# A two-layer trunk on one core: weights' splits held at the end of attention and of x's pairs, x loaded in four pieces, k's last part on VectorE

## Chip, core and metric

The kernel runs on one core of one Trainium2 chip. The metric is device time in microseconds (us) of one execution. All data are fp32 in HBM; the whole trunk runs in one launch.

## What is computed

A decoder trunk of two layers for one sequence of 256 positions, width 1024, feed-forward width 2816. Each layer adds half of a gated feed-forward block, then a mixer, then half of another feed-forward block; every block reads x through an RMS norm with its own gain, and a last norm follows. The mixer of layer 0 is, side by side, an attention of 8 heads of 64 whose three dilated windows are combined by their softmax sums, and a gated mixing of 4 groups of 128 positions by 128; layer 1 has a causal attention of 16 heads.

```
def swiglu(x, w_gate, w_up, w_down):
    return (jax.nn.silu(x @ w_gate) * (x @ w_up)) @ w_down
...
    h = x
    for layer in range(DEPTH):
        h = h + 0.5 * swiglu(rms_norm(h, ffn1_norm[layer]),
                             ffn1_w_gate[layer], ffn1_w_up[layer], ffn1_w_down[layer])
        hn = rms_norm(h, mix_norm[layer])
        if layer % 2 == 0:
            i = layer // 2
            h = h + ab_mixer(hn, ab_w_in[i], ab_v_norm[i], ab_w_spatial[i],
                             ab_b_spatial[i], ab_w_out[i])
        else:
            i = layer // 2
            h = h + c_mixer(hn, c_w_in[i], c_w_out[i])
        h = h + 0.5 * swiglu(rms_norm(h, ffn2_norm[layer]),
                             ffn2_w_gate[layer], ffn2_w_up[layer], ffn2_w_down[layer])
    return rms_norm(h, final_norm)
```

## The kernel before

**Engines.** TensorE (PE) multiplies and transposes, VectorE (DVE) and ScalarE (ACT) do the elementwise work, GpSimd (POOL) some of it, SyncE (SP) issues the loads.

**Three matmuls for one.** Each fp32 operand is split into a high part, rounded to the matmul's format, and a low part, the remainder. `mm3` (L223 to L226) multiplies high by high (L224), the weight's high by the other operand's low (L225), and the weight's low by the other's high (L226). For a 128 x 128 weight tile the moving operand has 256 columns, the positions.

**The weight stream.** `Stream` (L49 to L139) carries all weights through SBUF in chunks of 2048 columns by 128 partitions, 1 MB, in the order in which they are used. A chunk is loaded on SP's queue into one of 3 raw buffers (`load_one`, L72), then split by `split_one` into a high part (L105, ACT) and a low part (L106, DVE), in two or more pieces, into one of 4 pairs of buffers. `take` hands out the next chunk, `free` gives its buffers back, and both call `pump`, which issues every load and every split that the buffers allow at that point of the program. So a chunk's splits stand in the engines' order wherever a `free` happened to allow them. Chunks marked `reset` are laid out otherwise and split in more pieces (two of 384 columns first).

**Order on an engine.** The tile scheduler sets each engine's order, by the program's order and the dependences; only `begin` is written out by hand. `tc.issue_after` places the instructions that are made within it behind a given one on its engine.

**Phases.** ffn, mixer of layer 0 (`ab_mixer`), ffn, ffn, mixer of layer 1 (`c_mixer`), ffn. x is held transposed (features on partitions) as eight tiles of 128 x 256; `xTh` and `xTl` are its gained high and low parts for the next block. A block's norm is applied behind the matmuls, by `norm["row"]`, so that the next block's matmuls can begin before the sum of squares is known.

**End of a mixer.** `project` (L339 to L372) multiplies the mixer's output by w_out in two halves; each half fills two banks of PSUM, each bank a pair of x tiles. `Next.pair` (L265 to L289) takes such a pair: it adds x (L269, DVE), makes the two high parts (L259, ACT) and low parts (L262, DVE), squares (L279, ACT) and adds to the sum of squares (L283 to L289, DVE). The next ffn's first chunk (its order, `LATE`, leaves x's last two tiles for the end) starts right behind.

**Attention in `ab_mixer`.** `make_attention` (L623 to L714) gives five functions. `put_k` (L655) scales a pair of k heads (DVE), copies each head's high part (L661, ACT) and subtracts for its low part (L662, POOL). `scores` (L668) makes one head's scores (L677, L678, PE), adds the mask and takes the maximum (L681, DVE), exponentiates (L684, ACT), inverts the sum (L687, DVE) and scales (L691: POOL, but DVE for the last four heads). `turn` (L694) transposes a head's probabilities (L699, PE) and splits them (L229, ACT, and L230, DVE). `weighted` (L704) multiplies a pair of heads with v. `Slots` (L722) runs these at numbered steps of the projections' matmuls, so that PE has other work while a head goes through the engines: the last four heads' scores at 20, 20, 21, 21, their `turn` at 22, 22, 23, 23, and the last two `weighted` at 24 and 25, all within the first half of `project`.

**Begin.** `begin` (L375 to L456) loads x in rows of positions, as two tiles `xr`, and transposes it (L423) into four banks of two x tiles each; from these ACT and DVE take high and low parts (L259, L262) before any norm. Two halves of x's columns are loaded, each as two pieces of 128 x 512, ahead of the first and the third of four pieces of the first weight chunk. `heat` (L396) puts matmuls of zeros on PE; `turn_gains` (L401) transposes one of the three gain arrays and copies it (L405, DVE) into `gT`. Each of four steps waits for its two x tiles and its piece of the weight and does all three matmuls for them. The gains of the mixers and of the second ffn are transposed behind the third chunk of the first ffn.

Of the kernel before, what the change touches and what calls it, by code (L numbers as in the profile page):

```python
# [48 lines left out]
class Stream:  # L49


    def __init__(self, nc, pools):
        self.nc, (self.raw_pool, self.hi_pool, self.lo_pool) = nc, pools
        self.specs, self.raws, self.parts = [], {}, {}
        self.loaded = self.split = self.done = self.next = 0

# [62 lines left out]
    def pump(self):  # L119
        n = len(self.specs)  # L120
        while True:
            if self.loaded < n and self.loaded - RAW < self.split:
                self.load_one()
            elif self.split < self.loaded and self.split - SPL < self.done:
                self.split_one()
            else:
                break

# [14 lines left out]
def trunk(ctx: ExitStack, tc: tile.TileContext, a, out):  # L143
# [44 lines left out]
    add_ffn(a["ffn1_w_gate"][0], a["ffn1_w_up"][0], a["ffn1_w_down"][0], again=(1, 3, 5))  # L188
# [39 lines left out]
    def split(hi, lo, src):  # L228
        nc.scalar.activation(hi, src, AF.Copy)  # L229
        nc.vector.tensor_sub(lo, src, hi.bitcast(F32))  # L230
# [14 lines left out]
    class Next:  # L245
# [15 lines left out]
        def lo(self, k, src):  # L261
            nc.vector.scalar_tensor_tensor(xT["l"][:, k], src, self.gain(k), xT["h"][:, k].bitcast(F32),  # L262
                                           op0=ALU.mult, op1=ALU.subtract)

        def pair(self, i, p, row=None, pool=None):  # L265
# [10 lines left out]
            for k in (2 * i, 2 * i + 1):  # L276
                self.lo(k, X[:, k])
            q = wk.tile([128, 2, S], F32, name="sq" if i else "acc", bufs=1)
            nc.scalar.activation(q, xs, AF.Square, scale=1.0 / math.sqrt(D))  # L279
# [7 lines left out]
            if i == 3:  # L287
                for j in range(2):
                    nc.vector.tensor_add(f, f, q[:, j])  # L289

# [48 lines left out]
    def project(mix, order, phase, after):  # L339
# [35 lines left out]
    def begin(fp):  # L375

        nonlocal nxt
        xr = [fp.tile([128, D], F32, name=f"xr{t}") for t in range(NT)]
# [11 lines left out]
        nc.scalar.dma_start(*grs[0])  # L390
# [19 lines left out]
        for g in grs[1:]:  # L410
            nc.sync.dma_start(*g)
# [5 lines left out]
        p = bank()  # L417
        for i in range(4):
            if i < 2:
                for t in range(NT):  # L420
                    for k in range(4 * i, 4 * i + 4):
                        c = k % 2 * S + t * 128
                        nc.tensor.transpose(px[k // 2][:, c : c + 128], xr[t][:, k * 128 : (k + 1) * 128], ident)  # L423
                if i == 0:
                    heat(HEAT1)
            src = both(px[i])
            nxt.hi(2 * i, src[:, 0])
            nxt.lo(2 * i, src[:, 0])
            next(parts)
            nxt.hi(2 * i + 1, src[:, 1])  # L430
            nxt.lo(2 * i + 1, src[:, 1])
            w = st.parts[0]
            for k in (2 * i, 2 * i + 1):
                for j in range(2):
                    cs = slice(j * 128, (j + 1) * 128)
                    mm3(p[:, j * S : (j + 1) * S], w[0][k][:, cs], w[1][k][:, cs], xT["h"][:, k], xT["l"][:, k],
                        k == 0 and j == 0, k == KD - 1 and j == 1)
# [6 lines left out]
        for t in range(NT):  # L444
            xs = [xr[t][:, h * 512 : (h + 1) * 512] for h in range(2)]
# [10 lines left out]
        return p, turn_gains  # L456

    def ffn(phase):
        nonlocal nxt
        with tc.tile_pool(name="fp", bufs=1) as fp:  # L460
# [29 lines left out]
            for n in range(FT):  # L490
                k, m = n - n % 2, n % 2
                if phase == n == 0:
                    with tc.manual_schedule():
                        p, turn_gains = begin(fp)
# [10 lines left out]
                if phase == 0 and n == 2:  # L505
                    turn_gains(1)
                    turn_gains(2)
# [115 lines left out]
    def make_attention(mp, mask_cols, nheads, v, mix, rows=False):  # L623
# [31 lines left out]
        def put_k(p, bk):  # L655

            t = scaled(bk)
            for j in range(2):
# [3 lines left out]
                nc.gpsimd.tensor_sub(k[o, :], t[r, :], k[r, :].bitcast(F32))  # L662
# [5 lines left out]
        def scores(h):  # L668
# [10 lines left out]
            for b, (c0, n) in enumerate(((0, 128), (128, 256))):  # L679
# [4 lines left out]
                nc.scalar.activation(pr[:, cs], pr[:, cs], AF.Exp, bias=nm[:, b : b + 1], scale=-1.0,  # L684
                                     accum_out=l[:, b : b + 1])
            rl = wk.tile([128, 2], F32, name="rl")
            nc.vector.reciprocal(rl, l)  # L687
            for b, (c0, n) in enumerate(((0, 128), (128, 256))):
                cs = slice(c0, c0 + n)
                engine = nc.gpsimd if h < nheads - 4 else nc.vector  # L690
                engine.tensor_scalar(pr[:, cs], pr[:, cs], rl[:, b : b + 1], None, op0=ALU.mult)  # L691
            probs[h] = pr

        def turn(h):  # L694
# [7 lines left out]
            split(pts[p][0][:, j, :], pts[p][1][:, j, :], tp[:, :384])  # L702

        def weighted(p):  # L704
# [5 lines left out]
            for j in range(2):  # L710
                r = slice(j * 64, j * 64 + 64)
                split(mix[0][r, p], mix[1][r, p], o[r, j, :].rearrange("p (t c) -> p t c", t=NT))
# [86 lines left out]
    def ab_mixer(phase):  # L799
        with tc.tile_pool(name="mp", bufs=1) as mp:  # L800
# [142 lines left out]
```

## Time and profile before

| | us |
|---|---|
| median of 3 executions | 945.18 |
| lowest and highest | 945.04, 945.36 |
| the profiled execution | 944.62 |
| its span, first to last instruction | 942.9 |
| around the span | 1.72 |

The granted clock of TensorE was 0.999 over the span. The page of the profile gives busy times of PE (matmuls), PEld (weight loads, which overlap them), DVE, ACT, POOL and SP, counts behind an x, and groups of instructions by line of the program with their operands as output <- inputs. In a timeline a row is start, duration, engine, line, operation, operands, shape and count; in square brackets stands the idle time ahead of it and what ended it. In a list of waits the numbers are the total, the count and the longest. Matmuls overlap: a matmul's row lasts 0.28 us, but the next can start much earlier, so the distance between starts says how fast PE goes.

### The profile page before, as it was taken

Reading aid. Unit: us, or ns where it says so; the run is one execution under the profiler, and the core shown is the slowest. Engines: PE = TensorE matmul, PEld = TensorE weight load, DVE = VectorE, ACT = ScalarE, POOL = GpSimd, SP = SyncE. Lnnn points to the kernel's source line nnn. Section 1 sums busy time; section 2 is a strip of 40 time slices with the busy share of each in tenths; the row PEclk is TensorE's granted clock in tenths of the full one; section 3 lists DMA queues with packets and bytes.
Section 4 is the critical chain, followed back from the end, with each engine's and each line's share of the span. In section 5 each row is a group of like instructions: output and inputs, shape, how many; then the busy total and the mean of one; then the engine's idle time right before and its main releaser. Section 6 shows DMA issues by size and latency. Waiting matters only on the chain.

```text
span 942.9 us, 18152 instructions
## 1 busy us (share of the span) xinstructions
PE 933.5 (99%) x7685; PEld 911.5 (97%) x7685; DVE 607.5 (64%) x879; ACT 502.1 (53%) x790; POOL 83.4 (9%) x114
## 2 busy tenths in 40 slices
PE   9999999999999999999999999999999999999997
PEld 9999999999999999999999999999999999999886
DVE  6866556677886656655755665566787865666543
ACT  7754444468676445444554544456786755444431
POOL 0000000034400000000000000002574000000000
PEclk9999999999999999999999999999999999999999
DMA  9866555665447566556656655656544476556521
GB/s 305 277 207 196 172 194 172 224 221 179 135 135 221 182 185 210 176 170 203 220 180 188 210 184 171 197 186 215 178 136 136 133 230 195 179 180 201 201 90 44
DMA packets 153537, 174.86 MB, mean 185 GB/s; under 512 B 3008, under 2 KB 142192, under 8 KB 153456
## 3 DMA queue, kind: packets, MB, share of 16 engines
q1 hardware_dynamic: 151888, 171.54, 56.6%
q10 hardware_dynamic: 1568, 2.17, 0.7%
q8 instruction: 60, 0.98, 0.4%
q14 instruction: 21, 0.17, 0.0%
HBM read 172.65 MB, written 1.05 MB: 184 GB/s over the span
## 4 chain that ended last, share of the span: by engine, by line
PE 69%; DVE 2%; ACT 1%; issue 1%; POOLq 0%; POOL 0%; ACTq 0%
PE bank L224 21%; PE bank L225 21%; PE bank L226 20%; PE bank L545 2%; PE bank L549 2%; PE bank L546 2%; DVE wlo L106 1%; PE bank L699 1%; PE bank L677 0%; PE bank L678 0%; ACT whi L105 0%; DVE xTl L262 0%; PE bank L475 0%; DVE pr L691 0%; DVE pr L681 0%
## 5 line engine op out<-in xcount | busy, mean ns | idle before, releaser
L105 ACT ACTIVATE whi<-raw 128x1024 fp32r<-128x1024 f32 (+4 forms) x352 | 331.1, 985 | 366.1 <-issue 282.7
L106 DVE TENSOR_TENSOR wlo<-raw,whi 128x1024 fp32r<-128x1024 f32 (+4 forms) x352 | 390.3, 1141 | 134.9 <-ACT whi L105 133.7
L224 PE MATMUL bank<-xTh,whi 128*128 128x256 f32 x1632 | 452.5, 277 | 0.0
L225 PE MATMUL bank<-xTl,whi 128*128 128x256 f32 x1632 | 451.6, 277 | 0.3 <-DVE xTl L262 0.3
L226 PE MATMUL bank<-xTh,wlo 128*128 128x256 f32 x1632 | 451.2, 276 | 0.2 <-DVE wlo L106 0.2
L225 PEld LDWEIGHTS bank<-xTl,whi 128*128 128x128 f32 x1632 | 306.5, 188 | 0.9 <-DVE xTl L262 0.8
L226 PEld LDWEIGHTS bank<-xTh,wlo 128*128 128x128 f32 x1632 | 306.4, 188 | 0.6 <-DVE wlo L106 0.4
L224 PEld LDWEIGHTS bank<-xTh,whi 128*128 128x128 f32 x1632 | 306.5, 188 | 0.2 <-ACT whi L105 0.2
L224 PE MATMUL bank<-hTh,whi 128*128 128x256 f32 x528 | 145.7, 276 | 0.0
L225 PE MATMUL bank<-hTl,whi 128*128 128x256 f32 x528 | 145.7, 276 | 0.0
L226 PE MATMUL bank<-hTh,wlo 128*128 128x256 f32 x528 | 145.7, 276 | 0.0
L226 PEld LDWEIGHTS bank<-hTh,wlo 128*128 128x128 f32 x528 | 99.1, 188 | 0.0
L224 PEld LDWEIGHTS bank<-hTh,whi 128*128 128x128 f32 x528 | 99.1, 188 | 0.0
L225 PEld LDWEIGHTS bank<-hTl,whi 128*128 128x128 f32 x528 | 99.1, 188 | 0.0
L486 DVE TENSOR_TENSOR hm<-gs,bank 128x512 f32<-128x512 f32 x44 | 30.2, 687 | 79.7 <-PE bank L226 79.3
L483 DVE TENSOR_TENSOR gs<-bank,row 128x512 f32<-128x512 f32 x44 | 30.0, 689 | 47.7 <-PE bank L226 47.7
L224 PE MATMUL bank<-mixh,whi 128*128 128x256 f32 x128 | 35.2, 280 | 0.0
L225 PE MATMUL bank<-mixl,whi 128*128 128x256 f32 x128 | 35.1, 277 | 0.0
L226 PE MATMUL bank<-mixh,wlo 128*128 128x256 f32 x128 | 35.0, 277 | 0.0
L631 POOL MEMSET ql<- 64x256 f32 x12 | 3.7, 309 | 342.1 <-DVE x L273 341.7
L546 PE MATMUL bank<-wlo,hTh 128*128 128x512 f32 x80 | 31.1, 389 | 0.0
L545 PE MATMUL bank<-whi,hTh 128*128 128x512 f32 x80 | 31.1, 389 | 0.0
(139 smaller groups left out, 865.3 us busy)
## 6 DMA issues: line engine op xcount, KB each, us to landing
raw<-in_ffn_w_gate SPq DMA_DIRECT2D x42, 1024.0 KB, 5.3
raw<-in_ffn_w_up SPq DMA_DIRECT2D x42, 1024.0 KB, 5.4
raw<-in_ffn_w_down SPq DMA_DIRECT2D x35, 1024.0 KB, 5.1
raw<-in_c_w_in SPq DMA_DIRECT2D x12, 1024.0 KB, 5.2
raw<-in_ab_w_in SPq DMA_DIRECT2D x10, 1024.0 KB, 5.1
raw<-in_ffn_w_down SPq DMA_DIRECT2D x12, 768.0 KB, 4.5
raw<-in_ab_w_out SPq DMA_DIRECT2D x4, 1024.0 KB, 5.0
raw<-in_c_w_out SPq DMA_DIRECT2D x4, 1024.0 KB, 5.0
```

What stands on the lines that cost most here:

```text
L105: nc.scalar.activation(hi, r, AF.Copy)
L106: nc.vector.tensor_sub(lo, r, hi.bitcast(F32))
L224: nc.tensor.matmul(p, sh, mh, start=start, stop=False)
L225: nc.tensor.matmul(p, sh, ml, start=False, stop=False)
L226: nc.tensor.matmul(p, sl, mh, start=False, stop=stop)
L483: nc.vector.tensor_mul(g, both(pg), twice(norm["row"]))
L486: nc.vector.tensor_mul(hm, g, both(pu))
L545: nc.tensor.matmul(banks[t, h], sh, w[0][kw][:, cs], start=k == 0, stop=False)
L546: nc.tensor.matmul(banks[t, h], sh, w[1][kw][:, cs], start=False, stop=False)
L549: nc.tensor.matmul(banks[t, h], sl, w[0][kw][:, cs], start=False, stop=k == FT - 1)
L631: nc.gpsimd.memset(t[o, SHIFT + j * S : SHIFT + (j + 1) * S].bitcast(F32), 0.0)
L699: nc.tensor.transpose(tp[:, i * 128 : (i + 1) * 128], pr[:, i * 128 : (i + 1) * 128], ident)
```

## The change

It has five parts.

1. The stream can be held: `pump` then issues loads but no splits. `release` splits one chunk, or ends the hold, with the splits placed behind given instructions. In `ab_mixer` the stream is held from slot 19; one chunk is split behind the last head's exponential and scaling, one behind head 5's transposed split, and the rest behind the last `weighted`. In `project`, of both mixers, it is held before the third chunk is freed, and released behind the last pair's square and low part.
2. One chunk of the first ffn, the fourth, is split in two pieces of 1024 columns and no longer in four.
3. x is one tile, loaded in four pieces of 256 columns for both blocks of positions, one ahead of each piece of the first weight chunk. Two gain loads move from SP's queue to ACT's, at the start.
4. In `begin` the transposes of x stand two steps ahead of their use, a step's matmuls with the weight's low part stand behind the next transposes, the gains of the later blocks are transposed at the third step, and one transpose and one matmul of zeros go to a bank of their own at the end.
5. In `ab_mixer`, k's last pair is subtracted on DVE and no longer on POOL, and heads 4 and 5 are scaled on POOL and no longer on DVE.

```
+            elif not self.held and self.split < self.loaded and self.split - SPL < self.done:
                 self.split_one()
...
+    def hold(self):
+
+        self.held = True
+
+    def release(self, tc, behind, one=False):
+
+        with ExitStack() as s:
+            for b in behind:
+                s.enter_context(tc.issue_after(b.ins))
+            if one:
+                self.split_one()
+            else:
+                self.held = False
+                self.pump()
...
-    add_ffn(a["ffn1_w_gate"][0], a["ffn1_w_up"][0], a["ffn1_w_down"][0], again=(1, 3, 5))
+    add_ffn(a["ffn1_w_gate"][0], a["ffn1_w_up"][0], a["ffn1_w_down"][0], again=(1, 5))
...
         for pr in range(2):
             nxt.pair(pr, banks[pr])
+        st.hold()
         st.free()
         w = st.take()
         for pr in (2, 3):
...
-            nxt.pair(pr, banks[pr])
+            added = nxt.pair(pr, banks[pr])
+        st.release(tc, added)
         st.free()
...
         def load_x(i):
-            if i % 2 == 0:
-                h = i // 2
-                for t in range(NT):
-                    nc.sync.dma_start(xr[t][:, h * 512 : (h + 1) * 512],
-                                      x[t * 128 : (t + 1) * 128, h * 512 : (h + 1) * 512])
+            cs = slice(i * S, (i + 1) * S)
+            nc.sync.dma_start(xr[:, :, cs], x[:, cs].rearrange("(t p) c -> p t c", p=128))
...
-        nc.scalar.dma_start(*grs[0])
+        for g in grs:
+            nc.scalar.dma_start(*g)
...
+        turn_x(0)
+        heat(HEAT1)
+        turn_x(1)
         for i in range(4):
+            src = both(px[i])
+            for j in range(2):
+                nxt.hi(2 * i + j, src[:, j])
+            for j in range(2):
+                nxt.lo(2 * i + j, src[:, j])
+            next(parts)
+            w = st.parts[0]
+            tiles = [(k, j, p[:, j * S : (j + 1) * S], slice(j * 128, (j + 1) * 128))
+                     for k in (2 * i, 2 * i + 1) for j in range(2)]
+            for k, j, o, cs in tiles:
+                nc.tensor.matmul(o, w[0][k][:, cs], xT["h"][:, k], start=k == j == 0, stop=False)
+                nc.tensor.matmul(o, w[0][k][:, cs], xT["l"][:, k], start=False, stop=False)
             if i < 2:
...
+                turn_x(i + 2)
+            elif i == 2:
+                turn_gains(1)
+                turn_gains(2)
+            for k, j, o, cs in tiles:
+                nc.tensor.matmul(o, w[1][k][:, cs], xT["h"][:, k], start=False, stop=k == KD - 1 and j == 1)
+        e = bank()
+        nc.tensor.transpose(e[:, :128], warm, ident)
+        nc.tensor.matmul(e[:, 128:S], warm, ident, start=True, stop=True)
...
-                if phase == 0 and n == 2:
-                    turn_gains(1)
-                    turn_gains(2)
...
-                nc.gpsimd.tensor_sub(k[o, :], t[r, :], k[r, :].bitcast(F32))
+                engine = nc.vector if p == 3 and not rows else nc.gpsimd
+                engine.tensor_sub(k[o, :], t[r, :], k[r, :].bitcast(F32))
...
-                engine = nc.gpsimd if h < nheads - 4 else nc.vector
+                engine = nc.gpsimd if h < nheads - (4 if rows else 2) else nc.vector
...
-            slots.at((6, 7, 8, 9, 20, 20, 21, 21), scores)
-            slots.at((10, 10, 12, 12, 22, 22, 23, 23), turn)
-            slots.at((13, 14, 24, 25), weighted)
+            slots.at((19,), lambda _: st.hold())
+            slots.at((6, 7, 8, 9, 20, 20, 21), scores)
+            slots.at((21,), lambda _: st.release(tc, scores(7), True))
+            slots.at((10, 10, 12, 12, 22), turn)
+            slots.at((22,), lambda _: st.release(tc, turn(5), True))
+            slots.at((23, 23), lambda i: turn(6 + i))
+            slots.at((13, 14, 24), weighted)
+            slots.at((25,), lambda _: st.release(tc, weighted(3)))
```

`scores`, `turn`, `weighted`, `split` and `pair` now return the instructions behind which `release` places the splits.

More of the change, by code (lines that the diff above doesn't have):

```diff
@@ L289, in pair @@
                     nc.vector.tensor_add(f, f, q[:, j])
+            return square, low
         def sums(self):
@@ L417, in begin, with turn_x @@
         p = bank()
-        for i in range(4):
-            if i < 2:
[L420 to L437, printed above, removed]
+        def turn_x(i):
+            for k in (2 * i, 2 * i + 1):
+                for t in range(NT):
+                    c = k % 2 * S + t * 128
+                    nc.tensor.transpose(px[i][:, c : c + 128], xr[:, t, k * 128 : (k + 1) * 128], ident)
+        turn_x(0)
+        heat(HEAT1)
+        turn_x(1)
+        for i in range(4):
+            src = both(px[i])
[10 more added lines that the diff above has]
+                nc.tensor.matmul(o, w[0][k][:, cs], xT["l"][:, k], start=False, stop=False)
+            if i < 2:
+                turn_x(i + 2)
[7 more added lines that the diff above has]
+        nc.tensor.matmul(e[:, 128:S], warm, ident, start=True, stop=True)
         for _ in parts:
```

35 lines of the change are left out of this document (17 added, 18 removed).

## The prediction

> **What bounds the kernel now.** I read the page's span, engine shares and chain first, then what TensorE (PE) waited for, then its instructions one by one where it paused.
>
> ```profile
> span 942.9 us, 18152 instructions
> PE 933.5 (99%) x7685; PEld 911.5 (97%) x7685; DVE 607.5 (64%) x879; ACT 502.1 (53%) x790; POOL 83.4 (9%) x114
> PE 69%; DVE 2%; ACT 1%; issue 1%; POOLq 0%; POOL 0%; ACTq 0%
> ...
> PE bank L699 <- DVE pr L691: 1.3, 1, 1.3
> ...
> PE bank L225 <- DVE xTl L262: 0.3, 1, 0.3
> ```
>
> PE is busy 933.5 of 942.9 us. The change takes away no matmul, so all it can win lies in the other 9.4 us (some of it before the first transposes) and in stretches where PE counts as busy but issues at less than its pace. Those do not show as waits; they show as start-to-start distances. In the rows below (start, duration, engine) 282.43 to 282.77 is three matmuls: 0.113 us each, the pace of a fed PE.
>
> ```profile
> 262.49 0.82 PE L699 MATMUL bank<-ident,pr 128*128 128x128 f32 x6
> ...
> 263.27 0.28 PE L225 MATMUL bank<-mixl,whi 128*128 128x256 f32 x1
> ...
> 265.89 0.49 PE L699 MATMUL bank<-ident,pr 128*128 128x128 f32 x3
> 267.68 0.61 PE L699 MATMUL bank<-ident,pr 128*128 128x128 f32 x3 [1.29 <-DVE pr L691]
> ...
> 268.25 0.28 PE L225 MATMUL bank<-mixl,whi 128*128 128x256 f32 x1
> ...
> 282.43 0.28 PE L224 MATMUL bank<-xTh,whi 128*128 128x256 f32 x1
> ...
> 282.77 0.28 PE L224 MATMUL bank<-xTh,whi 128*128 128x256 f32 x1
> ...
> 284.10 0.28 PE L224 MATMUL bank<-xTh,whi 128*128 128x256 f32 x1
> ...
> 754.43 0.28 PE L224 MATMUL bank<-xTh,whi 128*128 128x256 f32 x1
> ...
> 755.51 0.28 PE L225 MATMUL bank<-xTl,whi 128*128 128x256 f32 x1
> ...
> 758.79 0.28 PE L226 MATMUL bank<-xTh,wlo 128*128 128x256 f32 x1
> ...
> 760.06 0.28 PE L224 MATMUL bank<-xTh,whi 128*128 128x256 f32 x1
> ```
>
> Four places: the transposes of heads 6 and 7 (265.89 to 268.25), and three where an FFN has just begun behind a mixer and reads x's last tiles.
>
> **Attention's end, A.** Six transposes and a matmul took 263.27 − 262.49 = 0.78 us for heads 4 and 5, and 268.25 − 265.89 = 2.36 for heads 6 and 7: 1.58 lost, to VectorE (DVE), which scaled head 7 late. The rows say with what it was busy:
>
> ```profile
> 262.78 1.22 DVE L106 TENSOR_TENSOR wlo<-raw,whi 128x1024 fp32r<-128x1024 f32 x1
> ...
> 267.25 0.55 DVE L691 TENSOR_SCALAR pr<-pr,rl 128x128 f32<-128x128 f32 x2
> ...
> L106 DVE TENSOR_TENSOR wlo<-raw,whi 128x1024 fp32r<-128x1024 f32 x12 | 14.4, 1219 | 3.5 <-ACT whi L105 3.4
> L230 DVE TENSOR_TENSOR ptl<-bank,pth 128x384 fp32r<-128x384 f32 x4 | 2.0, 548 | 0.0
> ...
> 253.97 1.54 POOL L662 TENSOR_TENSOR k<-qk,k 64x256 fp32r<-64x256 f32 x2 [0.33 <-ACT k L661]
> 255.73 2.28 POOL L662 TENSOR_TENSOR k<-qk,k 64x256 fp32r<-64x256 f32 x2 [0.22 <-ACT k L661]
> ...
> L691 POOL TENSOR_SCALAR pr<-pr,rl 128x256 f32<-128x256 f32 x16 | 17.8, 1112 | 0.0
> L691 POOL TENSOR_SCALAR pr<-pr,rl 128x128 f32<-128x128 f32 x16 | 10.1, 630 | 20.2 <-DVE rl L687 14.4 <-PE bank L699 5.5
> ```
>
> Two chunks' low halves, four L106 of 1.22 us (group mean 1219 ns), stood ahead of head 7's scaling, which ended at 267.25 + 0.55 = 267.80. With both chunks held that end moves to at most 267.80 − 4 × 1.22 = 262.9, 3.0 us before PE asks at 265.89: the whole 1.58 goes. Heads 4 and 5's scaling moves to POOL, 2 × (1.11 + 0.63) = 3.5 us; k's last two subtractions leave POOL (255.73 to 258.01), so I start it at 257.9 with head 4's sums and end near 261.4, against PE's 262.49: 1.1 us of cover. What was held must still be in time. The first chunk's splits run behind head 7's exponentials and scaling, by my count to 265.2, for a matmul at about 275. The second's stand behind head 5's transposes, to 268.3; the lows of heads 6 and 7 follow, 2 × 0.55 behind it, at 269.3, and the last `weighted` reads them, by my count, at about 270.7 (1.4 us of cover).
>
> The new cost is k's last two subtractions, on DVE from about 254.7, beside POOL's for the pair before (253.97 to 255.51), whose second part scores(5) waits for on PE. One POOL subtraction costs 1.54 / 2 = 0.77 with little beside it; the later two, 2.28 in all, ran partly beside a DVE L106. Two more of them undisturbed would be 1.54, so DVE cost POOL 0.74 there. DVE's two new ones are shorter than that L106: between nothing and 0.85 later; I take +0.25. A: −1.58 + 0.25 = **−1.33** (−1.58 to −0.73).
>
> The Trainium skill, SBUF — State Buffer, section Who interferes with whom, speaks against this edit: of a VectorE instruction with two SBUF inputs and a GpSimd one that reads SBUF, the second to come is blocked until the first has ended. L662's 2.28 beside L106 against 1.54 agrees. By that rule POOL's subtraction could wait for both of DVE's and A would be −0.73.
>
> **Pairs, B.** Distances against 0.113 per step: 282.77 to 284.10 is 9 steps, 1.33 − 1.02 = 0.31; 754.43 to 755.51 is 7, 1.08 − 0.79 = 0.29; 758.79 to 760.06 is 7 (one record is missing from the order L224, L225, L226), 1.27 − 0.79 = 0.48. Together 1.08, all where the lows of x's last pairs come late behind a chunk's splits:
>
> ```profile
> 756.46 2.42 DVE L106 TENSOR_TENSOR wlo<-raw,whi 128x384 fp32r<-128x384 f32 x3
> 758.80 0.87 DVE L262 SCALAR_TENSOR_TENSOR xTl<-x,gT,xTh 128x256 fp32r<-128x256 f32 x2
> ```
>
> Holding the next chunks until pair 3's low and square are issued puts this 2.42 behind the 0.87, so tile 7's low is ready near 756.46 + 0.87 = 757.3, and PE asks at 758.9. In the first mixer one chunk's lows (2 × 1.22) now stand ahead of the adds of pairs 0 and 1; I count pair 2's lows 0.45 us ahead of PE, the thinnest cover here, and if it fails the 0.31 stays or doubles. The held chunks end about 3 us ahead of their matmuls; their loads are issued up to 5 us later on SP, whose queue holds only loads, and the next chunk still lands 1 us or more before it is split. B: **−1.08** (−1.1 to −0.5).
>
> **The begin, C.** Rows: transposes, first matmul, the second weight chunk's first matmul, then the groups for 4 to 14 us (count, busy, mean ns), and the gains' place in the old order.
>
> ```profile
> 4.18 1.42 PE L423 MATMUL bank<-ident,xr 128*128 128x128 f32 x8
> ...
> 6.47 0.39 PE L224 MATMUL bank<-xTh,whi 128*128 128x256 f32 x1
> ...
> 13.78 0.28 PE L224 MATMUL bank<-xTh,whi 128*128 128x256 f32 x1
> ...
> 24.59 0.28 PE L226 MATMUL bank<-xTh,wlo 128*128 128x256 f32 x1
> ...
> 25.24 0.28 PE L225 MATMUL bank<-xTl,whi 128*128 128x256 f32 x1
> ...
> L262 DVE SCALAR_TENSOR_TENSOR xTl<-bank,gT,xTh 128x256 fp32r<-128x256 f32 x8 | 3.7, 480 | 2.3 <-ACT xTh L259 2.3
> L259 ACT ACTIVATE xTh<-bank,gT 128x256 fp32r<-128x256 f32 x8 | 3.6, 473 | 3.9 <-PE bank L423 3.6 <-DVE xTl L262 0.2
> ...
> L106 DVE TENSOR_TENSOR wlo<-raw,whi 128x512 fp32r<-128x512 f32 x4 | 2.8, 693 | 0.1
> ...
> L405 DVE COPY gT<-bank 128x16 f32<-128x16 f32 x1 | 0.2, 173 | 3.2 <-PE bank L404 3.2
> ```
>
> The 48 matmuls cost 48 × 0.113 = 5.4 us in either order, and the last eight transposes lie among them in either. What sets the end is DVE, with two lows and a split per step: 2 × 0.48 + 0.69 = 1.65, four times, 6.6 us. After: first transposes end near 5.15, the first high half 0.47 later, then 6.6, plus two gain copies that now stand in DVE's order (2 × 0.17): 12.6 if nothing else waits. The copies wait for PE's gain transposes, which stand behind the third step's matmuls, so I add 0.7: 13.3; then the last four matmuls and two fillers, 0.45 + 0.33: the next chunk starts near 14.1, +0.37. In return the gains leave 24.59 to 25.24, 0.65 for two steps of 0.23: −0.42. C: **0** (−0.6 to +0.6). x's four pieces are needed by PE at about 4.2, 5.9, 7.5 and 9.3. Before, x's second half, issued at 2.7 and 3.2, took 4.3 and 5.3 us to land (the row below: shortest, median, longest), at 7.0 and 8.5, and the same bytes lie ahead of it now:
>
> ```profile
> DMA to landing us min/median/max: 4.3/4.8/5.3
> ```
>
> so I count no wait for x. One chunk of the first FFN gets 2 + 2 splits for 4 + 4 on engines that are not the bound there: nothing. The two gain loads go from SP to ScalarE's queue, ahead of anything it does: nothing.
>
> **Sum.** −1.33 − 1.08 + 0 = −2.41. The profiled execution took 944.62 (span 942.9 and 1.72 around it), so 942.2 there; the median shown, 945.18, is 0.56 above it: **942.8**.
>
> **Rivals.** 1, **attention's wait is exchanged**: POOL, given heads 4 and 5 and slowed by DVE beside it, ends past 262.49, or its k subtraction is held by 0.85, and PE waits there in place of at head 7. For: 1.1 us of cover against POOL groups of 1.11 and 0.63. Against: POOL loses its 2.28 us of k. It leaves A at about −0.2 and the sum at −1.3: 943.9. 2, **x lands late**: PE's order now puts transposes of pieces 2 and 3 ahead of low-half matmuls, so a late piece stops ready ones. If pieces keep arriving 1.5 us apart, as those two did, the third comes some 1.2 us late: sum −1.2, 944.0. 3, **slower**: the start's transfers as a whole slow down, from runs of 1 KB in x's rows in place of 2 KB:
>
> ```profile
> 0.00:5.00 5.00, 3.90 (x17) 1.00 0.57 183
> 5.00:10.00 5.00, 4.77 (x40) 1.00 0.99 324
> 10.00:15.00 5.00, 5.00 (x43) 1.00 1.09 349
> ```
>
> (Length, PE busy and its count, granted clock, DMA share, GB/s of each stretch.) x, the first and the second weight chunk are 3.15 MB, and PE wants the last of it by about 13.6. From the first issue at 0.8 that is 246 GB/s on the mean, and below it PE waits: at 183 GB/s all the way they take 17.2 us, to 18.0, and PE stands 4.4 us: −2.4 + 4.4 = +2.0, 947.2. Against: 324 and 349 GB/s as soon as the queue is full. 4, **the begin gains**: with DVE and ACT fed earlier the step pauses (13.78 − 6.47 = 7.31, less 5.4 and 0.9 of transposes: 1.0 idle) vanish: −0.9 more, 941.9. 5, the order does not change what is late: 0, 945.2.
>
> **How the numbers follow.** The forecast 0.61; rival 1 0.12, rival 2 0.12, rival 4 0.08, rival 3 0.05, rival 5 0.02. The bounds of A, B and C added in the same direction would be −3.3 to −0.6; not all fall together. The range 941.2 to 944.4 takes in rivals 1, 2 and 4 and leaves out 3, 5 and the tails: about 2 in 10. About 0.2% (1.9 us) is what a measurement of this kernel can tell from no change, so faster means below 943.3: 0.53 of the forecast's own 0.61, and rival 4: 0.61. Within: the forecast's other 0.08 and rivals 1, 2 and 5: 0.34. Slower: rival 3, 0.05.
>
> **What would show it.** Right: transposes of heads 6 and 7 with no wait on DVE's pr (A); a wait of scores on POOL's k of some 0.25 us more; no wait on xTl behind either mixer and distances of 0.113 there (B); the second chunk's first matmul at 14.1, with DVE's gain copies followed by a pause of the fourth step, and no gain transposes near 24.6 (C). Wrong: PE waiting for POOL's pr of head 4 or 5 (rival 1), transposes waiting for x's pieces (2), the second chunk's matmuls waiting for its split behind a late landing (3), or the last `weighted` waiting for held lows, which I counted 1.4 us clear.

## The result and the profile after

The changed kernel takes 942.66 us (median of 10 executions, 942.21 to 943.19) against 945.2 (10, 944.85 to 945.88): ratio 0.9972, 95% interval 0.9962 to 0.9982, 2.54 us faster. The forecast was 942.8. Its profiled execution took 942.51, 2.11 less than the one shown of before. On the page, the share of DVE in the chain of work that ended last has gone from 2% to nothing.

```profile
span 940.8 us, 18159 instructions
PE 932.5 (99%) x7688; PEld 911.1 (97%) x7688; DVE 608.5 (65%) x875; ACT 501.8 (53%) x788; POOL 83.9 (9%) x116
...
PE 71%; issue 1%; ACT 0%; DVE 0%; POOL 0%; POOLq 0%
```

What PE waited for (total, times, longest): the waits on DVE's `pr` and `xTl` are gone, and two new ones stand in their place, on a piece of x and on POOL's k. The wait of 1.1 us at the start was there before.

```profile
PE bank L415 <- DVE warm L408: 1.1, 1, 1.1
PE bank L437 <- DMA xr<-in_x: 0.6, 1, 0.6
PE bank L702 <- POOL k L687: 0.3, 1, 0.3
```

**Where the time went.** The first products of gates and norm in each ffn (`gs`, on DVE) follow PE's matmuls without slack, so their starts say how far PE is, at four places: in the first ffn, behind the first mixer, in the third ffn, behind the second mixer. Before:

```profile
39.49 1.28 DVE L483 TENSOR_TENSOR gs<-bank,row 128x512 f32<-128x512 f32 x2
...
302.05 1.28 DVE L483 TENSOR_TENSOR gs<-bank,row 128x512 f32<-128x512 f32 x2
...
482.99 1.28 DVE L483 TENSOR_TENSOR gs<-bank,row 128x512 f32<-128x512 f32 x2
...
774.21 1.28 DVE L483 TENSOR_TENSOR gs<-bank,row 128x512 f32<-128x512 f32 x2
```

and after:

```profile
40.07 1.28 DVE L510 TENSOR_TENSOR gs<-bank,row 128x512 f32<-128x512 f32 x2
...
300.89 1.28 DVE L510 TENSOR_TENSOR gs<-bank,row 128x512 f32<-128x512 f32 x2
...
481.56 1.28 DVE L510 TENSOR_TENSOR gs<-bank,row 128x512 f32<-128x512 f32 x2
...
772.18 1.28 DVE L510 TENSOR_TENSOR gs<-bank,row 128x512 f32<-128x512 f32 x2
```

After less before is +0.58, −1.16, −1.43, −2.03. So the begin lost 0.58, the first mixer won 1.74, 0.27 came between the second and third ffn, where neither order nor work differs, and 0.60 came by the last place. These four differences, called offsets, are read for every kernel below, always against the one profile of before.

**At the places of the forecast.** PE's rows after: transposes of heads 4 and 5 (263.30) and of heads 6 and 7 (266.70) with the second matmul behind each, then the three places at the ffn's starts.

```profile
263.30 0.82 PE L725 MATMUL bank<-ident,pr 128*128 128x128 f32 x6
...
264.08 0.28 PE L241 MATMUL bank<-mixl,whi 128*128 128x256 f32 x1
...
266.70 0.82 PE L725 MATMUL bank<-ident,pr 128*128 128x128 f32 x6
...
267.48 0.28 PE L241 MATMUL bank<-mixl,whi 128*128 128x256 f32 x1
...
281.99 0.28 PE L240 MATMUL bank<-xTh,whi 128*128 128x256 f32 x1
...
283.01 0.28 PE L240 MATMUL bank<-xTh,whi 128*128 128x256 f32 x1
...
753.28 0.28 PE L240 MATMUL bank<-xTh,whi 128*128 128x256 f32 x1
...
754.08 0.28 PE L241 MATMUL bank<-xTl,whi 128*128 128x256 f32 x1
...
757.25 0.28 PE L242 MATMUL bank<-xTh,wlo 128*128 128x256 f32 x1
...
758.04 0.28 PE L240 MATMUL bank<-xTh,whi 128*128 128x256 f32 x1
```

Heads 6 and 7 now take the 0.78 us that heads 4 and 5 take. At the ffn's starts nine steps take 1.02 us, and seven take 0.80 and 0.79: all at 0.113 us per matmul. Now the begin, PE and then DVE:

```profile
6.80 0.63 PE L437 MATMUL bank<-ident,xr 128*128 128x128 f32 x4 [0.55 <-DMA xr<-in_x]
7.19 0.37 PE L453 MATMUL bank<-xTh,whi 128*128 128x256 f32 x1
...
14.73 0.37 PE L240 MATMUL bank<-xTh,whi 128*128 128x256 f32 x1
```

```profile
12.21 0.26 DVE L421 COPY gT<-bank 128x16 f32<-128x16 f32 x2 [1.01 <-PE bank L420]
```

PE goes on with x's second piece at 6.80, the first matmul comes at 7.19 and the second chunk's first at 14.73, not 14.1. The gain copies cost DVE 1.01 us of idle time.

**k's last pair** is now on DVE, beside the second subtraction of the pair before, which is POOL's. The rows are POOL's, DVE's two, and scores(5) on PE, which waits for POOL:

```profile
255.35 0.97 POOL L687 TENSOR_TENSOR k<-qk,k 64x256 fp32r<-64x256 f32 x1
```

```profile
255.31 0.42 DVE L687 TENSOR_TENSOR k<-qk,k 64x256 fp32r<-64x256 f32 x1 [1.04 <-ACT k L685]
...
255.76 0.84 DVE L687 TENSOR_TENSOR k<-qk,k 64x256 fp32r<-64x256 f32 x1
```

```profile
256.38 0.38 PE L702 MATMUL bank<-k,q 128*128 128x256 f32 x1 [0.32 <-POOL k L687]
```

### The profile page after: what moved, and what is told of

Same layout as the page of the kernel before. It is cut to its first block, busy times and chain, and to the rows that moved or that the text cites. A ratio compares the mean times of both kernels' runs of the same rounds, so it can differ in the third digit from the quotient of the medians.

```text
span 940.8 us, 18159 instructions
## 1 busy us (share of the span) xinstructions
PE 932.5 (99%) x7688; PEld 911.1 (97%) x7688; DVE 608.5 (65%) x875; ACT 501.8 (53%) x788; POOL 83.9 (9%) x116
## 4 chain that ended last, share of the span: by engine, by line
PE 71%; issue 1%; ACT 0%; DVE 0%; POOL 0%; POOLq 0%
PE bank L240 21%; PE bank L241 21%; PE bank L242 21%; PE bank L573 2%; PE bank L570 2%; PE bank L569 2%; PE bank L725 1%; PE bank L702 0%; PE bank L703 0%; PE bank L502 0%; PE bank L311 0%; ACT k L685 0%; DVE wlo L107 0%; ACT whi L106 0%; POOL k L687 0%
## 5 line engine op out<-in xcount | busy, mean ns | idle before, releaser
L240 PE MATMUL bank<-xTh,whi 128*128 128x256 f32 x1616 | 447.8, 277 | 0.0
L241 PE MATMUL bank<-xTl,whi 128*128 128x256 f32 x1616 | 446.5, 276 | 0.0
L242 PE MATMUL bank<-xTh,wlo 128*128 128x256 f32 x1616 | 446.4, 276 | 0.0
L241 PEld LDWEIGHTS bank<-xTl,whi 128*128 128x128 f32 x1616 | 303.4, 188 | 0.2
L716 POOL TENSOR_SCALAR pr<-pr,rl 128x128 f32<-128x128 f32 (+1 forms) x36 | 30.4, 858 | 23.9 <-DVE rl L712 16.9
```

The source lines that it names most:

```text
L240: nc.tensor.matmul(p, sh, mh, start=start, stop=False)
L241: nc.tensor.matmul(p, sh, ml, start=False, stop=False)
L242: nc.tensor.matmul(p, sl, mh, start=False, stop=stop)
L716: share = engine.tensor_scalar(pr[:, cs], pr[:, cs], rl[:, b : b + 1], None, op0=ALU.mult)
```

## The experiments

The theory is that the parts act apart, and that the sum is made of three terms: attention's hold (1.58 less what k's edit costs), the projections' hold, and a begin that does not pay. Each rival gives one of these terms another cause or another size. Totals are medians of the kernel and, in brackets, of the kernel before in the same comparison. The intervals are some 0.9 us wide to either side, so kernels of different comparisons are told apart by the steps between offsets more than by their totals.

| kernel | us (before) | ratio, 95% | offsets at the four places |
|---|---|---|---|
| after, profiled | 942.66 (945.2) | 0.9972, 0.9962 to 0.9982 | +0.58 −1.16 −1.43 −2.03 |
| old begin | 942.56 (945.28) | 0.9972, 0.9962 to 0.9982 | +1.08 −0.66 −0.92 −1.09 |
| no attention hold | 944.26 (945.28) | 0.9990, 0.9981 to 0.9999 | +0.73 +0.53 +0.28 −0.61 |
| k and scaling back | 942.77 (945.28) | 0.9973, 0.9963 to 0.9984 | +0.83 −1.15 −1.15 −1.77 |
| no hold in projections | 945.48 (945.28) | 1.0001, 0.9992 to 1.0011 | +1.39 +0.97 +0.73 +1.02 |
| new begin alone | 945.24 (945.0) | 1.0001, 0.9992 to 1.0009 | +1.02 +1.03 +0.77 +0.97 |
| gains last | 943.08 (945.0) | 0.9979, 0.9970 to 0.9988 | +0.66 −0.70 −0.96 −1.56 |
| second piece first | 942.78 (945.0) | 0.9975, 0.9966 to 0.9984 | +0.70 −0.65 −0.91 −1.08 |
| all three edits | 942.60 (945.0) | 0.9975, 0.9965 to 0.9984 | +0.41 −1.19 −1.19 −2.08 |
| holds alone | 941.83 (945.09) | 0.9965, 0.9953 to 0.9978 | +0.34 −1.60 −1.86 −2.73 |
| k's two pairs on VectorE | 941.96 (945.09) | 0.9968, 0.9955 to 0.9980 | +0.50 −1.44 −1.44 −2.05 |
| after again | 942.74 (945.09) | 0.9975, 0.9965 to 0.9985 | +0.48 −1.24 −1.50 −2.11 |
| two pairs and begin edits | 941.79 (945.09) | 0.9965, 0.9951 to 0.9978 | +0.93 −1.69 −1.93 −2.82 |

### The parts undone, one at a time

**Old begin.** `begin`, its gains, its loads and the fourth chunk's four splits are as before the change, and the rest is changed. Two lines of the edit:

```
-    add_ffn(..., again=(1, 5))
+    add_ffn(..., again=(1, 3, 5))
...
-                        p = begin(fp)
+                        p, turn_gains = begin(fp)
```

> The changed kernel with the old begin: x in the old pieces, transposes and gains at their old places, gain loads on SP, the fourth chunk split in four. Theory (the terms add; the new begin cost 0.58 us, because the second x piece lands later and the gain copies stop VectorE): the gates' products of the first ffn stand again where they stood before the change, and the whole takes 942.66 - 0.58 = 942.1 us. Rival (the new begin pays for itself later, by other starts of loads in the first ffn): no gain, 942.7 or more.

942.56 lies between the theory's 942.1 and the rival's 942.7, and can't be told from 942.66. In its profiled execution the offset is +1.08 with the old begin, worse than after's +0.58; but that execution, 943.49, was 0.93 above the kernel's median. Most of the offset arises behind the begin: at 14 us PE stood at +0.3. PE's windows of this kernel (length, busy and count, clock, DMA share, GB/s):

```profile
17.00:24.00 7.00, 7.00 (x62) 1.00 1.06 339
27.00:35.00 8.00, 8.00 (x71) 1.00 0.99 305
```

and of the changed kernel, the same windows:

```profile
17.00:24.00 7.00, 7.00 (x64) 1.00 1.06 343
27.00:35.00 8.00, 8.00 (x73) 1.00 1.03 323
```

There are 62 and 71 matmuls for 64 and 73, at a granted clock of 1.00 in both: from about 15 to 36 us most matmuls started 0.118 us apart (the expectations call it 0.117) and not 0.113, which is 0.74 of the 1.08. A second such stretch, from about 743 to 764 us, costs 0.7 ahead of the last place. So the offsets of two profiles can differ by more than half a microsecond without any difference in the work.

**No attention hold.**

```
-            slots.at((19,), lambda _: st.hold())
-            slots.at((6, 7, 8, 9, 20, 20, 21), scores)
-            slots.at((21,), lambda _: st.release(tc, scores(7), True))
...
+            slots.at((6, 7, 8, 9, 20, 20, 21, 21), scores)
+            slots.at((10, 10, 12, 12, 22, 22, 23, 23), turn)
+            slots.at((13, 14, 24, 25), weighted)
```

> The changed kernel without the hold at attention's end (the hold in the projections, k on VectorE and heads 4 and 5 on POOL stay). Theory (the hold is what brings head 7's scaling forward): the transposes of heads 6 and 7 wait for VectorE again, 1.2 to 1.6 us are lost between heads 4 and the last weighted, total 944.0 to 944.3. Rival (the moves of k and of the scaling freed enough of VectorE by themselves, 4 x 0.3 us of scaling): at most 0.5 us lost, total below 943.2.

944.26, as the theory had it. Head 7's wait is back, with k and the scaling still moved:

```profile
268.59 0.61 PE L725 MATMUL bank<-ident,pr 128*128 128x128 f32 x3 [1.18 <-DVE pr L716]
```

The first mixer wins only 0.20 (+0.73 to +0.53). The moves alone do almost nothing for heads 6 and 7, whose transposes and matmul take 2.25 us against 2.36 before. And without the hold POOL's scaling of heads 4 and 5 ends at 263.83, inside their transposes, which begin at 263.22 and with their matmul take 1.06 in place of 0.78: a small piece of rival 1, which did not come where attention's hold stands.

**k and scaling back.**

```
-                engine = nc.vector if p == 3 and not rows else nc.gpsimd
+                engine = nc.gpsimd
...
-                engine = nc.gpsimd if h < nheads - (4 if rows else 2) else nc.vector
+                engine = nc.gpsimd if h < nheads - 4 else nc.vector
```

> The changed kernel with k's last pair on POOL again and heads 4 and 5 scaled on VectorE again; the holds stay. Theory (the k edit costs 0.23 us by blocking POOL's subtraction for the pair before, and the hold alone frees VectorE): scores(5) starts 0.2 us earlier against the matmuls ahead of it, head 7's transposes do not wait, total 942.4. Rival (the hold needs the moves, since POOL's k for heads 6 and 7 then delays nothing but VectorE's scaling of four heads comes late): the transposes of heads 4 to 7 wait 0.3 us or more, total 943.0 or more.

The first mixer wins 1.98 in place of 1.74, 0.24 more, without a wait at heads 4 to 7. The median, 942.77, does not show it. In the profiled execution, 942.83, the begin stands 0.25 later than after's (PE waits 1.3 us for x's second piece), and the 0.27 between second and third ffn is missing. The theory's step holds; its total, 942.4, did not come.

**No hold in the projections.**

```
-        st.hold()
         st.free()
...
-        st.release(tc, added)
         st.free()
```

> The changed kernel without the hold in the projections (attention's hold stays). Theory (the hold in the projections gains 0.39 behind the first mixer and 0.60 behind the second): waits on xTl come back behind both mixers, 0.9 to 1.1 us lost, total 943.6 to 943.8. Rival (the chunks freed late by attention's hold keep the first mixer's pairs clear anyway): only the second mixer loses, 0.6, total 943.3.

945.48: both expectations fail, for the loss is 2.8 and not 1.0. The last two places tell that the second mixer's gain is gone, as expected. The rest is the first mixer: it wins 0.42 in place of 1.74. Attention's part of that is still won, since PE stands at +0.03 at 275 us, from +1.39; but 0.94 of it is lost again by 290 us. DVE there:

```profile
282.38 1.49 DVE L107 TENSOR_TENSOR wlo<-raw,whi 128x1280 fp32r<-128x1280 f32 x1
283.78 1.28 DVE L284 TENSOR_TENSOR x<-bank,x 128x512 f32<-128x512 f32 x2
```

and PE:

```profile
285.06 0.50 PE L240 MATMUL bank<-xTh,whi 128*128 128x256 f32 x2 [0.74 <-ACT xTh L274]
```

The chunks that attention held back are split among x's pairs, the largest piece of a chunk's low part (1280 of 2048 columns, 1.49 us) ahead of the last adds, and PE waits for x's high part. Attention's hold alone moves its splits into the pairs: there it gives back most of what it won. The two holds are one change. The begin at +1.39 goes with x's second piece, which let PE go on at 7.63 in this profile, 0.83 later than in after's.

### The begin

**New begin alone** (`begin`, `again=(1, 5)` and the gains of the change in the kernel before).

> The kernel before with the new begin alone (x in four pieces, transposes two steps ahead, gains at the third step, the fourth chunk in two splits); attention and projections as before. The profiled pair of before and after differ by +0.58 us at the first ffn's products, but the kernel with the old begin and everything else new took 942.56 against 942.66, and its profiled run stood 0.5 us later there than after's, half of it or more by matmuls going at 0.117 us in place of 0.113 for 30 us. Theory (the two begins cost the same within what executions differ): 945.2, within 0.3 us. Rival (the new begin costs its 0.58 us): 945.8.

945.24 against 945.0: the same, within the interval, though its profile stands at +1.02, with two waits of PE for pieces of x, 0.6 us together.

**Gains last**, and **second piece first**:

```
-            elif i == 2:
-                turn_gains(1)
-                turn_gains(2)
...
-        e = bank()
-        nc.tensor.transpose(e[:, :128], warm, ident)
-        nc.tensor.matmul(e[:, 128:S], warm, ident, start=True, stop=True)
+        turn_gains(1)
+        turn_gains(2)
```

```
-            cs = slice(i * S, (i + 1) * S)
-            nc.sync.dma_start(xr[:, :, cs], x[:, cs].rearrange("(t p) c -> p t c", p=128))
+            for cs in [slice(j * S, (j + 1) * S) for j in ((0, 1), (), (2,), (3,))[i]]:
+                nc.sync.dma_start(xr[:, :, cs], x[:, cs].rearrange("(t p) c -> p t c", p=128))
```

> The changed kernel with the later gains transposed behind the fourth step and no longer at the third, and without the two fillers of zeros. Theory (the gain copies, which wait for TensorE, hold VectorE 1.0 us idle, and the fourth step's low halves and its split come that much late): VectorE goes on with the fourth step's lows at 11.2 in place of 12.4, no pause in the fourth step, the second weight chunk's first matmul 0.4 us earlier in the same state of the loads, total 942.2. Rival (TensorE's own order sets the end of the begin, and the pause only fills what it has): within 0.15 us of 942.66.

> The changed kernel with x's second piece loaded right behind the first, ahead of the first weight piece; nothing else differs in any engine's order. Theory (x's second piece, which lands at 6.7 us, stops the transposes for 0.55 us and with them the first matmuls, which were otherwise ready at 6.7): the second piece lands near 5, no wait for x, first matmul at 6.7 to 6.9 in place of 7.2, total 942.2. Rival (what the second piece gains the first weight piece loses, or the second transfer is late whatever it carries): first matmul no earlier than 7.1, total 942.66 within 0.2.

**Gains last** came to 943.08, neither the theory's 942.2 nor the rival's 942.66 within 0.15. The order does what the theory said of it: DVE's pause moves behind the fourth step, and the second chunk's first matmul comes at 13.90, 0.83 us earlier than after's. But the third one waits for the split of that chunk:

```profile
13.90 0.39 PE L240 MATMUL bank<-xTh,whi 128*128 128x256 f32 x1
14.12 0.28 PE L241 MATMUL bank<-xTl,whi 128*128 128x256 f32 x1
14.72 0.39 PE L242 MATMUL bank<-xTh,wlo 128*128 128x256 f32 x1 [0.32 <-DVE wlo L107]
```

By the first place nothing is left: +0.66 against after's +0.58. **Second piece first** came to 942.78, and its rival held: x's second piece, now second in the queue, lands 3.4 us after its issue in place of 4.9 and no longer stops PE, but the first weight piece, now third, takes 4.8 and does (its high half starts on ACT at 6.61, when it lands). The first matmul comes at 7.30, not 6.8.

**All three edits**: these two, and k and the scaling as before.

> The changed kernel with the three edits together: k's last pair on POOL and heads 4 and 5 scaled on VectorE as before the change, the later gains behind the fourth step without the fillers, x's second piece ahead of the first weight piece. Theory (the three terms add: -0.24, -0.4, -0.4): 941.6, below both kernels. Rival (the begin's two edits share one cover, since an earlier start only meets VectorE's queue): 942.1.

942.60, neither the theory's 941.6 nor the rival's 942.1, and no better than the changed kernel, although its begin stands at +0.41. What the order on PE wins at the begin, DVE's queue of lows and splits takes back. The first mixer wins only 1.60 here, because a stretch at 0.118 us from about 255 us on lies in it; so k's 0.24 can be seen neither in this profile nor between the totals.

**After again**, the changed kernel unchanged.

> The changed kernel itself once more, to tell what differs from execution to execution of one kernel. Theory (the time of x's second piece and the pace of the matmuls, 0.113 or 0.117 us over stretches of up to 30 us, differ by execution): 942.3 to 943.0 on the median, and in its profile the first ffn's products stand elsewhere than at +0.58 us against the profile before, or a stretch at 0.117 us lies elsewhere. Rival (both belong to the kernel): the profile repeats after's within 0.05 us at the first ffn, and the same stretches.

942.74 against 942.66. This time x's second piece landed 4.2 us after its issue and not 4.9, and PE had no need to wait for it:

```profile
6.32 0.60 PE L437 MATMUL bank<-ident,xr 128*128 128x128 f32 x4
```

The first matmul came at 6.74 in place of 7.19. But at 8.06 PE waited 0.11 for the third piece, the second chunk began at 14.63 against 14.73, and the first offset moved by 0.10 only, to +0.48. That the landing of x's pieces differs by execution is shown. Of the pace it is the rival that held: the steps between the four places are 1.72, 0.26 and 0.61 against 1.74, 0.27 and 0.60, and the two windows above hold 64 and 73 matmuls again. So whether a stretch at 0.118 us belongs to the kernel or to the execution stays open. The only kernel with two profiles has the same ones in both, while the totals of one kernel spread by up to 1.6 us (941.35 to 942.99 for k's two pairs on VectorE).

### What suffices, and what is left

**Holds alone**: of the change only `hold` and `release`, in attention and in the projections.

> The kernel before with nothing of the change but the two holds (attention's end and the projections); k's last pair on POOL, heads 4 and 5 scaled on VectorE, the begin and the fourth chunk as before. Theory (the whole gain is the holds': 1.58 us at head 7 and 1.2 us at the pairs): 942.5, no wait of the transposes on VectorE, scores(5) not later than before. Rival (the begin or the moves of k and of the scaling carry part of it): 943.0 or more.

941.83 (five executions, 941.79 to 941.87): lower than the theory's 942.5, and faster than the changed kernel in every execution of the same comparison (942.41 to 943.01). The first mixer wins 1.94, the second 0.87. Heads 6 and 7 on PE:

```profile
266.25 0.82 PE L719 MATMUL bank<-ident,pr 128*128 128x128 f32 x6
...
267.03 0.28 PE L241 MATMUL bank<-mixl,whi 128*128 128x256 f32 x1
```

The whole gain is the holds'; the begin, x's pieces and the moves of k and of the scaling add nothing, and k's costs. At the last place this kernel stands 0.70 ahead of after's profile: 0.24 from the begin, 0.20 from the first mixer and 0.26 from the second, where the changed kernel has a wait that is looked at below. Set beside "k and scaling back", which differs from it in the begin and the fourth chunk alone, it is 0.94 faster (0.75 when each is taken against its own before).

**k's two pairs on VectorE**, and the same with the **begin edits**:

```
-                engine = nc.vector if p == 3 and not rows else nc.gpsimd
+                engine = nc.vector if p > 1 and not rows else nc.gpsimd
```

> The changed kernel with k's last two pairs subtracted on VectorE, and none of them on POOL. Theory (VectorE and POOL stop each other only while both subtract; on VectorE alone a subtraction is 0.42 us in place of POOL's 0.73, and VectorE stands idle there): scores(4) and scores(5) on TensorE start 0.3 and 0.7 us earlier against the matmuls ahead of them, total 942.0. Rival (the scaling of the last pair's k, which now stands behind these subtractions on VectorE, makes the exponentials of heads 4 and 5 1.3 us later, and the transposes of head 4 or 5 wait for POOL's scaling): a wait of the transposes of 0.5 us or more, total 942.7 or more.

> The same as the kernel with k's last two pairs on VectorE, with the later gains behind the fourth step, no fillers, and x's second piece ahead of the first weight piece. Theory (the begin is set by VectorE's lows and splits and not by the order of TensorE or of the pieces, as the two earlier runs showed): within 0.3 us of the kernel without these begin edits, 942.0. Rival (the earlier x piece counts once TensorE's pause is gone): 941.6.

The first came to 941.96, as its theory had it, and the second to 941.79, between its theory's 942.0 and its rival's 941.6. In the second the first mixer wins 2.62, 0.88 more than the changed kernel's 1.74 and 0.68 more than the holds alone: the two subtractions of a pair take 0.87 us on DVE together, POOL has none beside them, and scores(4) and scores(5) follow each other at full pace, four matmuls in 0.46 us:

```profile
254.78 0.87 DVE L683 TENSOR_TENSOR k<-qk,k 64x256 fp32r<-64x256 f32 x2 [0.48 <-ACT k L681]
```

```profile
255.51 0.28 PE L698 MATMUL bank<-k,q 128*128 128x256 f32 x1
...
255.97 0.28 PE L698 MATMUL bank<-k,q 128*128 128x256 f32 x1
```

The first of the two shows less on its offsets because its profile has a stretch at 0.118 us from about 271 to 292, which costs 0.70. The wait of the first one's rival did not come. The second (941.43 to 942.03) and the holds alone are below every execution of the changed kernel in the same comparison; the first overlaps them (941.35 to 942.99 against 942.41 to 943.01). Among themselves the three can't be told apart. The holds with k's two pairs on VectorE and the old begin were not run.

## Why the prediction was right

**A, attention's end: right, in mechanism and size.** The forecast took 1.58 for head 7; with the holds alone PE stands at −1.22 at 275 us, from +0.34 at the first place: 1.56. It took +0.25 for k; scores(5) came 0.23 late (256.38 against 255.57, less the 0.58 of the begin), and 0.24 returned with the edit undone. The net is 1.36 (the first mixer's 1.74 less 0.38 at its pairs) against 1.33. Head 7's scaling on DVE

```profile
263.19 0.55 DVE L716 TENSOR_SCALAR pr<-pr,rl 128x128 f32<-128x128 f32 x2
```

ended at 263.74, 3.0 us ahead of 266.70, as worked out. POOL's scaling of heads 4 and 5 had more cover than forecast: it

```profile
258.51 3.00 POOL L716 TENSOR_SCALAR pr<-pr,rl 128x128 f32<-128x128 f32 x4 [2.19 <-DVE rl L712]
```

ended at 261.51 against 263.30, 1.8 us and not 1.1. Rival 1 did not come.

On k, the Trainium skill, SBUF — State Buffer, section Who interferes with whom, states that a VectorE instruction with two SBUF inputs contends with a GpSimd one that reads SBUF. The trace agrees in kind: POOL's subtraction took 0.97 in place of the 0.73 of the one before it, and DVE's second 0.84 in place of the first's 0.42, each longer by no more than one instruction of the other engine. So it looks as if the two took turns. The −0.73 that the forecast worked out from that rule did not come: POOL lost 0.24 and not the length of both of DVE's.

**B, the pairs: right, a little small.** 1.08 was forecast; 0.38 came behind the first mixer and 0.88 behind the second, 1.26 in all. The 0.88 is the step from the third to the fourth place in four profiles: without the attention hold, all three edits, holds alone, two pairs and begin edits (0.87 to 0.89). The changed kernel's own 0.60 is 0.88 less 0.28, and that 0.28 is a wait ahead of the pairs, in the second mixer's attention. By the profile an exponential of one of its later heads, on ScalarE, waits there for POOL's k, and not for DVE's maximum as before; what follows on ScalarE and DVE comes 0.28 later against PE, and one set of six transposes takes 1.09 and not 0.82. ScalarE before, then ScalarE and PE after:

```profile
729.29 0.40 ACT L684 ACTIVATE pr<-pr,nm 128x128 f32<-128x128 f32 x1 [1.62 <-DVE nm L681]
```

```profile
728.15 0.40 ACT L709 ACTIVATE pr<-pr,nm 128x128 f32<-128x128 f32 x1 [1.90 <-POOL k L687]
```

```profile
737.72 1.09 PE L725 MATMUL bank<-ident,pr 128*128 128x128 f32 x6
```

The same wait of 1.90 stands in the second profile of the changed kernel and in those of k and scaling back, no hold in projections, gains last and k's two pairs; the other kernels have 1.62. Nothing in the change is aimed at this place, and why the wait is in some programs and not in others stays open. The rest that was missed is small delays spread over the steps beside the three places. What the forecast did not see is that B is not a term of its own: without it most of A is lost again behind attention.

**C, the begin: the sizes were off, and the net is not settled.** The step that failed is "x's four pieces are needed by PE at about 4.2, 5.9, 7.5 and 9.3 [...] so I count no wait for x". The landings that it leaned on were those of x's second half; none was worked out for the second piece, which landed 4.9 us after its issue at 1.79. PE's order put that piece's transposes ahead of every matmul, so it went on at 6.80 and the first matmul came at 7.19, against 6.47 before. The pause for the gain copies, put in at 0.7, was 1.01. So the second chunk began 0.95 later, not 0.37 (the forecast's own 14.1 less 13.78 is 0.32); the gains' old place gave back 0.37 of the 0.42. That is rival 2 at the second piece and not the third: PE stood 0.55 us for it, about half the rival's price. In the other profile of the changed kernel it was the third piece, with 0.11.

Against the one profile of before all this is +0.58, but that execution was 0.56 under its median, and the two other kernels with the old begin reached their second chunk 0.30 and 0.35 later than it. The totals do not settle it: the new begin alone costs 0.24 (from −0.8 to +0.9 by its interval), the old begin in the changed kernel is 0.10 faster, and between k and scaling back and the holds alone it is 0.75 to 0.94. So C's zero can't be told from half a microsecond of loss, and no total shows a gain. That the total came within 0.14 of the forecast is partly luck: in the profiled pair C was off by 0.58, and B's surplus and a slow stretch in the profile of before made up for about half of it.

**Rival 3** did not come: the first three stretches of 5 us moved 174, 301 and 353 GB/s against 183, 324 and 349. But ACT waited 0.45 us for the second chunk's last half, so its cover was as thin as worked out.

**The sum.** 942.2 was forecast for the profiled execution, and 942.51 came, 0.3 more: C +0.58, B −0.18, A −0.03, −0.27 by the pace between second and third ffn, +0.28 by the wait ahead of the second mixer's pairs, and −0.08 behind the last place.

## What to carry to other kernels

When one engine is busy 99% of the time, what can still be won may be found in the distances of its starts, and its cause in another engine's order: here it was background work that a buffer's release happened to place ahead of a late, short result. Holding that work back was worth the whole delay when it was held past the next such result too; held only past the first, it fell on the second. Two profiles of one kernel agreed within 0.02 us in the steps behind the begin and differed by 0.10 at the begin, but totals of one kernel spread by up to 1.6 us: for a difference of half a microsecond compare the steps, or several executions.

## What was not expected of the hardware

- The same matmuls start 0.113 us apart in one stretch and 0.118 in another, at a granted clock of 1.00 in both (64 against 62 in 7 us). A stretch lasted up to some 20 us and lay elsewhere in other kernels; in the profile of before one runs from about 466 to 473 us, which is the 0.27 that the changed kernel seemed to win there. Each moved the offsets by up to 0.74 us. What sets it was not tried.
- Two engines that subtracted at the same time seem to have taken turns, one instruction each: 0.97 for 0.73 on POOL, 0.84 for 0.42 on DVE.
- A piece of 256 KB that was asked for at 1.8 us, third in the queue, landed 4.9 us later in one execution of the changed kernel and 4.2 in another; second in the queue it took 3.4, and the weight piece that was third then took 4.8.
